# Sparse attention output with channels on partitions: three branches in one PSUM accumulation, gates applied to the probabilities

## The chip, the core and the metric

The kernel runs on one core of a Trainium2 chip. A core has five engines that matter here: TensorE (PE, matrix products and transposes; PEld is its weight load), VectorE (DVE), ScalarE (ACT), GpSimd (POOL) and SyncE (SP), which here only issues DMAs. Each engine works through its own list of instructions in order and waits on semaphores for the others. The metric is the device time of one execution in microseconds; smaller is better. Before the change the median of three runs is 2396.43 us (2393.08 to 2398.14).

## The reference, cut to what matters

The kernel computes two layers over 1024 tokens of 1024 channels, all in fp32. Layer 0 (retention and mLSTM heads) is not touched. Layer 1 has 16 heads of sparse attention (NSA, four groups of four heads, 64 channels a head) beside an S5 part. NSA has three branches: compressed blocks (c), selected blocks (s) and a window of 512 tokens (w). Each has its own softmax, and the outputs are added with a gate each, then multiplied by the output gate and sent through the output projection:

```python
p_c = jax.nn.softmax(s_c, axis=-1)
o_c = jnp.einsum('bgktj,bjgd->btgkd', p_c, vc)
...
p = jax.nn.softmax(s.reshape(b_, g, hpg, Q_BLOCK, topn * SEL_BLOCK), axis=-1).reshape(s.shape)
o_s = jnp.einsum('bgkqns,bgqnsd->bqgkd', p, v_sel)
...
p_w = jax.nn.softmax(s_w, axis=-1)
o_w = jnp.einsum('bgkqs,bsgd->bqgkd', p_w, vwb)
...
gt = jax.nn.sigmoid(gate_pre).reshape(b_, s_, g, hpg, 3)
o = gt[..., 0:1] * o_c + gt[..., 1:2] * o_s + gt[..., 2:3] * o_w
...
y_nsa = y_nsa * jax.nn.silu(nz)
mix = jnp.concatenate([y_nsa, y_s5], -1).astype(u.dtype)
return mix @ w_out
```

## The kernel before

**Products in two parts.** Each fp32 operand of a large product is split into a high part that the matrix unit takes exactly and a low part (`hi` by ACT, `lo` by a subtraction on DVE or POOL), and a product is three matmuls: high by high, high by low, low by high. `load_w` (lines 148 to 166) does this for weights: a DMA into one of two `raw` buffers, then a slot of the pool `wsp`, which has six slots of `whi` and six of `wlo`.

**Projections of layer 1.** The generator `nsa_projections` computes queries, keys, values, the branch gates and the output gate of NSA and writes them to DRAM; it yields after each group of products, and its pieces are used as work for PE inside other stages. Values are one product of 512 columns per tile of 128 tokens (8 tiles of 24 matmuls). Branch gates (48 columns) and output gate (1024 columns) are three products of 360, 356 and 356 columns per tile (`proj_tok`, L1099 to L1111): tokens on partitions. They go to DRAM as `gD` and `zD`, row by row of tokens; `gts` brings the branch gates back.

**Units.** The attention is 32 units: four groups gg of heads by eight tiles i of 128 tokens. A unit runs through these steps:

- `head` (L1310): loads the queries, computes the compressed scores (tile `cs`) and their softmax (`scc`, on DVE and ACT), the mask `mg` of the selected blocks (POOL), transposes the four heads' probabilities (`ct`, L1363), splits them (`cp`) and multiplies them with the compressed values, four matmuls of 128 columns (`co`), which ACT copies to `o6`. It is issued one unit ahead.
- `scores` (L1402) for the window and then for the selected branch: per head two matmuls for up to 512 keys (`sc`), a DVE instruction that adds the mask and finds the maximum (L1415, tiles `pr` and `nm`), and an ACT exponential that also gives the sum (L1418, `sums`). The probabilities `pr` stay unnormalised.
- `values` (L1423) for each branch: per 128 keys four transposes on PE into one PSUM tile (`pt`, L1429), a split (`pthh` by ACT, L1398; `pthl` by DVE, L1399), and two matmuls of 512 columns into the accumulator `av`, which has one buffer. Channels stand on its partitions, high and low part of the values in its halves. ACT and DVE add the halves into `ob` (L1437, L1438) at the end of each branch.
- the end of a unit: four transposes of `ob` back to tokens on partitions (`ot`, L1591), an ACT copy (L1592), a reciprocal of the eight sums and the factors `cf` (L1594 to L1597, DVE and POOL), the sum of the halves of the compressed branch (L1599, DVE), then L1600 to L1604 on POOL: two multiplications by the factors, two additions, and the product with the output gate `zn`. The result goes to DRAM as `mixN`, tokens by channels.

**Filler.** `filler` is a generator with S5's GLU (`gl`) and the output projection (`fp`, three groups of k-tiles, and the last one with the norm). `step` takes pieces from it between the steps of a unit, by credits that the table `share` sets per group. NSA tiles are read back from `mixN` and transposed (`turn`, tile `ft`, L1458), split (`fhi`, `flo`), and multiplied.

**Order.** The program is written in Python order and then put into each engine's order by a scheduler, by a simulated time of its own; so an edit moves instructions on all engines. After the units, `gate_stage` (products `gp`) ends the kernel; `late_tile` does the last NSA tile there.

Of the kernel before, what the change touches and what calls it, by code (L numbers as in the profile page):

```python
# [33 lines left out]
def shape_constants():  # L34
    """Arrays that depend on the shapes alone, packed along one row of 128 partitions."""
# [62 lines left out]
def body(tc, A, out, dbg=None):  # L98
# [69 lines left out]
    def chunk(w, segs, nkt=8, kt0=0, gain=None, pack=True):  # L168
        """[kt pair] high and low parts; four k-tiles share a slot where the columns are few"""
# [5 lines left out]
    def proj_tok(ps, uT, i, ck, n, c0=0, nkt=8, start=True, stop=True):  # L175
        """ps[tokens of tile i, n] = u @ W"""
# [9 lines left out]
    def proj_col(ps, uT, half, ck, c0, m=128, nkt=8):  # L186
        """ps[m columns, 512 tokens] = (u @ W).T"""
# [20 lines left out]
    def transpose_split(x, i, hi, lo, nk=8, off=None):  # L208
        """x [128 tokens, nk*128] -> hi/lo[:, k, tokens]"""
# [31 lines left out]
    zD = dram.tile([S, S], FT, name="zD")  # L241
    mixN = dram.tile([S, S], FT, name="mixN")
# [34 lines left out]
    # ------------------------------------------------------------- layer 1: S5 matrices of the parameters  # L277
    def s5_prepare(e):
# [43 lines left out]
        # turns by 1..8 chunks (fine) and by 0, 8, .. 120 chunks (rough); sines of the lower half negated  # L322
# [10 lines left out]
        def rotate(oc, os, xc, xs, yc, ys, tmp):  # L333
            """(oc, os) = (xc, xs) turned by (yc, ys)"""
# [7 lines left out]
        def double(X, o, m, n):  # L342
            """entries o+n.. o+n+m-1 = entries o .. o+m-1 turned by entry o+n-1"""
# [14 lines left out]
        # (abar - 1) / a  # L358
# [13 lines left out]
        # B and i*B, stacked [re; im]  # L372
# [17 lines left out]
        # C, conjugated and stacked: cc = [re; -im], jc = [-im; -re]  # L390
# [68 lines left out]
    # ------------------------------------------------------------- layer 0: retention heads  # L459
# [8 lines left out]
    def halve(hi, lo, src, eng=v):  # L468
        """src as exact high and low parts"""
# [11 lines left out]
    def gate_z(z_ps, dst):  # L481
        """dst = z*(1+tanh(z/2)) = 2*silu(z)"""
# [3 lines left out]
    def values_in(ck, n, extra=None):  # L486
        """the value rows' parts, tile by tile"""
# [16 lines left out]
    def cell(c, scf, q, kz, vc, st, n, decay):  # L504
        """one chunk: its output in PSUM and the next state"""
# [20 lines left out]
    def retention_head(h):  # L526
# [43 lines left out]
        # mix  # L570
# [134 lines left out]
    def mlstm_keys(h):  # L705
        """queries and keys after the convolution"""
# [19 lines left out]
    def mlstm_head(h, qk, V):  # L726
# [44 lines left out]
        # gates of the cell's output and of the head  # L771
# [75 lines left out]
    def square_weights(w, ext, gain=None, kt0=0, nkt=8):  # L847
        """[col half][kt pair] slots of nkt*128 rows of a 1024-column matrix"""
# [6 lines left out]
    def in_pairs(front, proj, after=None, order=tuple(range(NT))):  # L855
        """Tiles two by two, the left column halves first; a tile's front runs a tile or two ahead."""
# [21 lines left out]
    def out_stage(pw, src, w, kt0, ext, gain, sink, nkt=8, after=None):  # L878
        """sink(i, half, psum) for src @ (gain * w[kt0*128..])"""
# [14 lines left out]
    def post_norm(pw, i, y, gpost, resid, dst):  # L894
        """dst rows = resid rows + rmsnorm(y) * gpost"""
# [10 lines left out]
    def gate_stage(pw, layer, ext, src, dst, nxt=None, ppD=None, order=tuple(range(NT)), ph=None, late=()):  # L906
        """dst = h + sigmoid(h Wg) * (p Wp); with nxt, also the next layer's normalised input"""
# [55 lines left out]
        def turn(i):  # L963
            """the next layer's input: norm of tile i, transposes of tile i - 1"""
# [716 lines left out]
```

## Time and profile before

| what | value |
|---|---|
| time, median of 3 runs | 2396.43 us |
| span of the profiled execution | 2390.1 us |
| PE busy in it | 2311.4 us (97%) |
| DVE, ACT, POOL busy | 1448.3, 1047.9, 426.3 us |
| attention stage, 1567 to 2278 us | 711 us, PE busy 674.05 us |

The span is the time from the first to the last instruction of one execution that the hardware profiler took; the runs' times are measured from outside and are some 6 us longer. "Busy" of PE is the time covered by matmul records. These records include the time a matmul takes to drain, so that they overlap: the true cost of one matmul in a dense stretch is the distance from its start to the start of the next. A row of the time line gives a start, a duration and a count; the distance of two rows' starts divided by the count is that cost.

### The profile page before, as it was taken

The numbers are of one execution on the slowest core, as the hardware profiler recorded it, in microseconds if no ns is written. First come the engines' busy times: TensorE is split into PE (matmuls) and PEld (weight loads), VectorE is DVE, ScalarE is ACT, GpSimd is POOL, SyncE is SP. The second block draws the span as 40 slices with busy tenths as digits, with TensorE's granted clock in tenths as the row PEclk, the third lists the DMA queues.
The fourth block names the chain that finished last, engine by engine and source line by source line (L and its number), as shares of the span: only waits on it lengthen the run. The fifth ranks groups of instructions, "written<-read, shape, count | busy, mean of one in ns | idle before, by whom it ended". The sixth has DMA issues, their size and how long they took to land. (4 is left out here: it accounts for less than half of the span.)

```text
span 2390.1 us, 34752 instructions
## 1 busy us (share of the span) xinstructions
PE 2311.4 (97%) x12230; PEld 1940.6 (81%) x12230; DVE 1448.3 (61%) x3760; ACT 1047.9 (44%) x2271; POOL 426.3 (18%) x618
## 2 busy tenths in 40 slices
PE   7999999999999999899999999989999999999888
PEld 6878789788887888788888868979888888887767
DVE  6777647755554334343387332357768878898933
ACT  6233323433332331223332212256777877777821
POOL 0122200000000000100000000023444244445610
PEclk9999999999999999999999999999999999999999
DMA  5323312021111645314377412452363353435542
GB/s 158 90 80 103 100 45 71 27 80 35 55 57 50 242 153 213 112 69 132 116 224 240 118 46 102 121 150 76 106 188 119 99 158 102 137 120 174 165 139 112
DMA packets 255609, 279.69 MB, mean 117 GB/s; under 512 B 54688, under 2 KB 190344, under 8 KB 255402
## 3 DMA queue, kind: packets, MB, share of 16 engines
q1 hardware_dynamic: 242858, 242.05, 32.8%
q10 hardware_dynamic: 8960, 26.49, 3.2%
q0 software_dynamic: 3616, 8.92, 1.3%
q8 instruction: 97, 1.59, 0.3%
q14 instruction: 78, 0.64, 0.1%
HBM read 190.03 MB, written 88.62 MB: 117 GB/s over the span
## 5 line engine op out<-in xcount | busy, mean ns | idle before, releaser
L139 PE MATMUL pj<-whi,uh 128*128 128x512 f32 (+2 forms) x768 | 278.5, 363 | 2.6 <-ACT whi L163 1.1
L139 PE MATMUL pj<-wlo,uh 128*128 128x512 f32 (+2 forms) x768 | 277.7, 362 | 0.0
L139 PE MATMUL pj<-whi,ul 128*128 128x512 f32 (+2 forms) x768 | 277.7, 362 | 0.0
L1418 ACT ACTIVATE pr<-pr,nm 128x640 f32<-128x640 f32 (+7 forms) x256 | 187.7, 734 | 44.3 <-DVE nm L1415 43.4
L1399 DVE TENSOR_TENSOR pthl<-pt,pthh 128x512 fp32r<-128x512 f32 x264 | 176.4, 683 | 20.1 <-ACT pthh L1398 18.7
L164 DVE SCALAR_TENSOR_TENSOR wlo<-raw,gnp,whi 128x512 fp32r<-128x512 f32 (+4 forms) x248 | 142.3, 610 | 72.8 <-ACT whi L163 70.2
L139 PE MATMUL gp<-whi,mhl 128*128 128x512 f32 x512 | 167.8, 403 | 7.0 <-DVE mhl L219 4.9
L163 ACT ACTIVATE whi<-raw,gnp 128x512 fp32r<-128x512 f32 (+4 forms) x248 | 135.2, 605 | 75.7 <-PE pj L139 38.8
L139 PEld LDWEIGHTS pj<-whi,uh 128*128 128x128 f32 x768 | 145.6, 190 | 26.0 <-ACT whi L163 1.4
L139 PE MATMUL op<-whi,mhl 128*128 128x512 f32 x520 | 165.0, 395 | 0.9 <-ACT mhl L218 0.9
L1398 ACT ACTIVATE pthh<-pt 128x512 fp32r<-128x512 f32 x264 | 150.8, 594 | 32.3 <-PE pt L1429 28.2
L1429 PE MATMUL pt<-consts,pr 128*128 128x128 f32 x1056 | 157.0, 275 | 7.8 <-ACT pr L1418 6.1
L139 PEld LDWEIGHTS pj<-wlo,uh 128*128 128x128 f32 x768 | 145.7, 190 | 22.8 <-issue 0.7
L139 PEld LDWEIGHTS pj<-whi,ul 128*128 128x128 f32 x768 | 145.3, 189 | 22.3 <-issue 0.2
L139 PE MATMUL pj<-vh,whi 128*128 128x512 f32 x384 | 153.0, 399 | 0.2 <-ACT vh L218 0.2
L1429 PEld LDWEIGHTS pt<-consts,pr 128*128 128x128 f32 x1056 | 128.9, 142 | 29.5 <-ACT pr L1418 7.8
L139 PE MATMUL pj<-vl,whi 128*128 128x512 f32 x384 | 151.4, 394 | 0.0
L139 PE MATMUL pj<-vh,wlo 128*128 128x512 f32 x384 | 150.8, 393 | 0.0
L139 PE MATMUL sc<-kh,q 128*128 128x320 f32 (+5 forms) x384 | 139.3, 366 | 5.8 <-DVE nm L1415 5.3
L139 PE MATMUL sc<-kl,q 82*128 82x320 f32 (+5 forms) x384 | 126.3, 332 | 0.0
L139 PEld LDWEIGHTS gp<-whi,mhl 128*128 128x128 f32 x512 | 97.3, 191 | 29.5 <-DVE mhl L219 5.4
L139 PE MATMUL av<-pthl,vt 128*128 128x512 f32 x264 | 112.8, 427 | 4.1 <-DVE pthl L1399 3.6
(439 smaller groups left out, 5658.0 us busy)
## 6 DMA issues: line engine op xcount, KB each, us to landing
raw<-in_ab_w_in_dram SPq DMA_DIRECT2D x100, 256.0 KB
yD<-fy SPq DMA_DIRECT2D x48, 256.0 KB
raw<-in_cd_w_in_dram SPq DMA_DIRECT2D x20, 512.0 KB
raw<-in_ab_w_out_dram SPq DMA_DIRECT2D x16, 512.0 KB
raw<-in_pe_gate_dram SPq DMA_DIRECT2D x16, 512.0 KB
qD<-qst SPq DMA_DIRECT2D x16, 512.0 KB
q<-qD SPq DMA_DIRECT2D x32, 256.0 KB
fin<-yD SPq DMA_DIRECT2D x32, 256.0 KB
```

The source lines that it names most:

```text
L139: return t.matmul(o, l, r, start=start, stop=stop, **k)
L163: s.activation(hi[:, k], raw[:, k], AF.Copy, scale=gain(kt0 + k))
L164: v.scalar_tensor_tensor(lo[:, k], raw[:, k], gain(kt0 + k), hi[:, k].bitcast(FT), op0=OP.mult, op1=OP.subtract)
L1398: s.activation(hi[:dst_shape], ps[:dst_shape], AF.Copy)
L1399: v.tensor_tensor(lo[:dst_shape], ps[:dst_shape], hi[:dst_shape].bitcast(FT), op=OP.subtract)
L1418: s.activation(pr[:, :nk], pr[:, :nk], AF.Exp, scale=-1.0, bias=nm[:, c:c + 1], accum_out=sums[:, b, h:h + 1])
L1429: t.transpose(ps[:, h * 128:(h + 1) * 128], P[h][:, k * 128:(k + 1) * 128], ident)
```

## The change

The output of a unit stays with channels on partitions, and all three branches are added up in `av`.

- The probabilities are scaled before the transposes: `scale` (new) takes the reciprocal of the four sums of a branch and multiplies by the gate (two DVE instructions on 128x4), then POOL multiplies each head's `pr` by its factor, in place. There are 256 such POOL instructions, 128 to 1024 columns wide, 135168 columns in all. The compressed probabilities are multiplied by their gate on POOL (`sg`).
- The four `co` matmuls and their ACT copy become one matmul of 512 columns that opens the accumulation in `av`; `values` of both branches add to it. The halves are added once, 64x256 twice where it was 64x512 twice.
- `ot`, its ACT copy, L1594 to L1597 and L1599 to L1603 are gone. The product with the output gate remains.
- `zD` and `mixN` are channels by tokens. The output gate is computed with channels on partitions (`proj_col`, two chunks of 512 columns, 384 matmuls of 512 columns); the branch gates come with the selected values (304 columns), window values apart (256 columns), and stay in SBUF (`gates`, no `gD`).
- The filler reads `mixN` with channels on partitions already, so `turn` goes away for NSA tiles: it splits straight from SBUF (ACT and POOL). It now waits in its generator until the units it reads are written.
- Two heads are issued at other places (n in (3, 8) for (3, 11)), the first group of keys at n == 11, and `share` is {30, 26, 20, 64} for {30, 30, 28, 66}.

```diff
+            sg = nh.tile([128, 4, 64], FT, name="sg", tag="sg", bufs=1)
+            g.tensor_tensor(sg, sc, gate_of(gg, i)[:, 0, :, None].to_broadcast([128, 4, 64]), op=OP.mult)
...
-            ps = pC.tile([128, 512], FT, name="co", tag="pc")
-            for h in range(4):
-                hs = slice(h * 128, (h + 1) * 128)
-                mm(ps[:, hs], pc2[:, hs], vcT[:, gg, :], True, True)
-            s.activation(o6[:, 0].rearrange("p h d -> p (h d)"), ps, AF.Copy)
-            return q2, q3, o6, mg
+            return q2, q3, pc2, mg
...
+        def scale(P, nk, b, sums, gv):
+            cf = nh.tile([128, 4], FT, name="cf", tag="cf", bufs=4)
+            v.reciprocal(cf, sums[:, b])
+            v.tensor_tensor(cf, cf, gv[:, 1 + b], op=OP.mult)
+            for h in range(4):
+                g.tensor_scalar(P[h][:, :nk], P[h][:, :nk], cf[:, h:h + 1], None, op0=OP.mult)
...
-                T = turn(x, 2)
+                T = local_parts(x, 2, g)
...
             Pw = scores(K[1], q2, q3, i, 1, None, sums)
+            scale(Pw[0], Pw[2], 1, sums, gv)
             step(gg, nw / 2)
             Ps = scores(K[0], q2, q3, i, 0, mg, sums)
+            scale(Ps[0], Ps[2], 0, sums, gv)
             step(gg, ns / 2)
-            values(K[1], *Pw, ob, 1)
+            acc = pV.tile([128, 512], FT, name="av", tag="av")
+            mm(acc, vcT[:, gg, :], pc2, True, False)
+            values(K[1], *Pw, acc, False)
             step(gg, nw / 2)
-            values(K[0], *Ps, ob, 0)
+            values(K[0], *Ps, acc, True)
             step(gg, ns / 2)
-            ps = pT.tile([128, 512], FT, name="ot", tag="pt")
-            for h in range(4):
-                t.transpose(ps[:, h * 128:(h + 1) * 128], ob[:, h * 128:(h + 1) * 128], ident)
...
+            for b, here, there in ((0, lo_, up), (1, up, lo_)):
+                s.activation(oc[here], a4[there, :, b], AF.Copy)
+                v.tensor_tensor(ob[here], a4[here, :, b], oc[here], op=OP.add)
+            (g if n + 1 < len(units) else v).tensor_tensor(zt, zt, ob, op=OP.mult)
```

How this moves instructions is shown at two places. The first is PE at the end of a unit. Before, a unit's end reads like this (`ot` are the transposes back, `pt` those of the next unit's probabilities, `ft` the filler's, `ct` the compressed branch's):

```order
L1458 MATMUL ft_18009<-consts_75,fin_18007 128x128 x2
L1363 MATMUL ct_18074<-consts_75,scc_18049 64x128 x4
L139 MATMUL sc_18151<-kh_14698,q2_17693 128x448
L139 MATMUL sc_18151<-kl_14699,q3_17694 128x448
L139 MATMUL sc_18158<-kh_14698,q2_17693 128x448
L139 MATMUL sc_18158<-kl_14699,q3_17694 128x448
L1591 MATMUL ot_18016<-consts_75,ob_17750 128x128 x4
L1429 MATMUL pt_18209<-consts_75,pr_18091 128x128
```

In the changed program the same place has no `ot`; three `pt` tiles of the window are filled head by head, the next unit's scores (`sc`, `cs`) and the filler (`fp`) stand between, and the accumulation `av` opens with one matmul of the compressed branch (`cp` by `vcT`):

```order
L1438 MATMUL pt_17726<-consts_75,pr_17625 128x128
L1438 MATMUL pt_17737<-consts_75,pr_17625 128x128
L1438 MATMUL pt_17748<-consts_75,pr_17625 128x128
L139 MATMUL sc_17938<-kh_14645,q2_17552 128x320
L139 MATMUL sc_17938<-kl_14646,q3_17553 128x320
L139 MATMUL fp_16936<-whi_16880,fhi_16896 128x512
L139 MATMUL sc_17942<-kh_14645,q2_17552 128x320
L139 MATMUL sc_17942<-kl_14646,q3_17553 128x320
L139 MATMUL cs_17891<-kcH_12067,q2_17886 128x64
L139 MATMUL av_17724<-cp_17285,vcT_12069 128x512
```

The transposes of the sum left PE's row, and the transposes of the probabilities (`pt`) now read what POOL has scaled. The second place is POOL in the middle of a unit of the third group. Before, its row holds the mask `mg` and the end of the unit (`o6`, `zn`):

```order
L1358 COPY mg_17410<-i2_17407 128x640
L1359 TENSOR_TENSOR mg_17410<-i2_17407,c_scaus_12058 128x128
L1600 TENSOR_TENSOR o6_17377<-o6_17377,cf_17749 128x4x64
L1601 TENSOR_TENSOR o6_17111<-o6_17111,cf_17428 128x512
L1602 TENSOR_TENSOR o6_17111<-o6_17111 128x4x64
L1596 COPY cf_18089<-gts_12071 128x4
L1345 MEMSET im_18972 128x18
L1603 TENSOR_TENSOR o6_17111<-o6_17111 128x4x64
```

In the changed program it holds the scaling of the window's four heads and of the selected branch's four heads, with two weight splits (`wlo`) and the output gate's product (`zn`) between them:

```order
L1365 TENSOR_TENSOR mg_17589<-i2_17586,c_scaus_12057 128x128
L1431 TENSOR_SCALAR pr_17603<-pr_17603,cf_17647 128x640
L1431 TENSOR_SCALAR pr_17614<-pr_17614,cf_17647 128x640
L1431 TENSOR_SCALAR pr_17625<-pr_17625,cf_17647 128x640
L1431 TENSOR_SCALAR pr_17636<-pr_17636,cf_17647 128x640
L160 TENSOR_TENSOR wlo_16881<-raw_16879,whi_16880 128x1024
L160 TENSOR_TENSOR wlo_16887<-raw_16885,whi_16886 128x1024
L1607 TENSOR_TENSOR zn_17236<-zn_17236,ob_17543 128x256
L1431 TENSOR_SCALAR pr_17663<-pr_17663,cf_17707 128x768
L1431 TENSOR_SCALAR pr_17674<-pr_17674,cf_17707 128x768
```

POOL was at the end of a unit's chain; now it stands in the middle, between the exponentials and PE's transposes.

## Rows read from the trace of the kernel before

**Rows 1.** The page's busy time of each engine: us, share, instructions.

```profile
PE 2311.4 (97%) x12230; PEld 1940.6 (81%) x12230; DVE 1448.3 (61%) x3760; ACT 1047.9 (44%) x2271; POOL 426.3 (18%) x618
```

**Rows 2.** Busy time of engines in the attention stage; clock, DMA share, GB/s.

```profile
1567.00:2278.00 711.00, 674.05 (x4087) 576.34 (x4086) 580.99 (x1688) 530.96 (x1158) 310.72 (x390) 0.98 0.44 135
```

**Rows 3.** PE's waits in that stage: us in total, times, longest us.

```profile
PE ot L1591 <- DVE ob L1438: 6.2, 7, 2.0
PE pt L1429 <- ACT pr L1418: 6.1, 5, 4.9
...
PE co L139 <- DVE cp L1366: 3.1, 2, 2.1
```

**Rows 4.** Time line of PE inside units: start us, us, instruction, count.

```profile
1818.81 0.64 PE L139 MATMUL co<-vcT,cp 128*128 128x128 f32 x4
1819.29 0.41 PE L1458 MATMUL ft<-consts,fin 128*128 128x128 f32 x2
1819.45 0.39 PE L139 MATMUL sc<-kh,q 128*128 128x320 f32 x1
...
1825.19 0.39 PE L139 MATMUL av<-pthh,vt 128*128 128x512 f32 x1
1825.42 0.40 PE L139 MATMUL av<-pthl,vt 128*128 128x512 f32 x1
...
1831.44 0.66 PE L1591 MATMUL ot<-consts,ob 128*128 128x128 f32 x4 [0.29 <-DVE ob L1438]
1831.94 1.04 PE L1429 MATMUL pt<-consts,pr 128*128 128x128 f32 x8
```

**Rows 5.** Time line of PE in dense products of 512, 356, 256 columns.

```profile
1440.15 0.40 PE L139 MATMUL pj<-whi,vh 128*128 128x512 f32 x1
...
1445.76 0.40 PE L139 MATMUL pj<-whi,vh 128*128 128x512 f32 x1
...
1554.75 0.33 PE L139 MATMUL pj<-whi,vl 128*128 128x356 f32 x1
...
1558.67 0.33 PE L139 MATMUL pj<-whi,vl 128*128 128x356 f32 x1
...
1598.65 0.28 PE L139 MATMUL gl<-flo,whi 128*128 128x256 f32 x1
...
1599.96 0.28 PE L139 MATMUL gl<-fhi,whi 128*128 128x256 f32 x1
```

**Rows 6.** POOL's groups by shape: count, busy us, mean ns of one.

```profile
L1519 POOL TENSOR_TENSOR fy<-fy,fin 128x512 f32<-128x512 f32 x32 | 41.2, 1287 | 80.8 <-ACT fy L1515 78.5 <-DVE scc L1337 2.3
...
L1602 POOL TENSOR_TENSOR o<-o 128x256 f32<-128x256 f32 x31 | 22.9, 738 | 1.6
...
L1358 POOL COPY mg<-i 128x896 f32<-128x896 f32 x4 | 3.7, 930 | 0.4 <-DVE i L1354 0.2
...
L1358 POOL COPY mg<-i 128x256 f32<-128x256 f32 x4 | 1.6, 397 | 0.3
```

**Rows 7.** DVE's and ACT's groups by shape, on the units' path.

```profile
L1438 DVE TENSOR_TENSOR ob<-av,oc 64x512 f32<-64x512 f32 x64 | 44.0, 687 | 9.7 <-ACT oc L1437 8.4
L1415 DVE CUSTOM_DVE_ANT_0 pr<-sc,c_wmask,nm 128x320 f32<-128x320 f32 x64 | 34.8, 543 | 7.3 <-PE sc L139 6.4
...
L1447 DVE TENSOR_TENSOR flo<-ft,fhi 128x256 fp32r<-128x256 f32 x23 | 9.5, 415 | 0.4 <-ACT fhi L1446 0.3
...
L1334 DVE RECIPROCAL m<-m 128x4 f32<-128x4 f32 x32 | 5.5, 171 | 0.5
...
L1418 ACT ACTIVATE pr<-pr,nm 128x640 f32<-128x640 f32 x80 | 66.3, 828 | 21.5 <-DVE nm L1415 21.2
L1418 ACT ACTIVATION_READ_ACCUMULATOR pr<-pr,nm 128x1 f32 x256 | 49.2, 192 | 0.0
```

**Rows 8.** DVE on tile cf (durations min/median/max ns), POOL on line 160 (mean ns).

```profile
L1597 DVE TENSOR_TENSOR cf<-sums,gts x32: 130/168/1734, 1589.8 to 2264.6; 128x8 f32<-128x8 f32 x32
...
L160 POOL TENSOR_TENSOR wlo<-raw,whi 128x1024 fp32r<-128x1024 f32 x20 | 47.5, 2384 | 66.8 <-PE sc L139 38.1 <-ACT whi L159 24.0 <-PE gl L139 2.6
```

More of the change, by code (lines that the diff above doesn't have):

```diff
@@ L240, in body @@
     aqD = dram.tile([NA, 16, S], FT, name="aqD")
-    zD = dram.tile([S, S], FT, name="zD")
-    mixN = dram.tile([S, S], FT, name="mixN")
+    zD = dram.tile([8, 128, S], FT, name="zD")
+    mixN = dram.tile([8, 128, S], FT, name="mixN")
     mixS = dram.tile([512, 8, 128], FT, name="mixS")
@@ L1048, in body @@
     NL = 1
-    gD = dram.tile([128, 8, 48], FT, name="gD")
     uD = dram.tile([512, 8, 128], FT, name="uD")
@@ L1054, in body @@
     pz = [(psA, "psA")]
+    gates = [None]
     def nsa_projections(pd):
@@ L1431, in values @@
                 vb = K[2][:, k0 // 128 + k, :]
-                mm(acc, vb, hi, k == 0, False)
-                pace[0] = mm(acc, vb, lo, False, k == n - 1)
-            lo_, up = slice(0, 64), slice(64, 128)
-            here, there = (up, lo_) if b else (lo_, up)
-            oc = n2.tile([128, 512], FT, name="oc", tag="oc", bufs=1)
-            s.activation(oc[here], acc[there], AF.Copy)
-            v.tensor_tensor(ob[here], acc[here], oc[here], op=OP.add)
+                mm(acc, vb, hi, False, False)
+                pace[0] = mm(acc, vb, lo, False, last and k == n - 1)
         def filler():
@@ L1496, in filler @@
                                               (A["p"][1, 0], A["pe_proj"][1], 0, 2, ppD, False),
[L1497 to L1498 removed]
+                                              (mixN, W2, 0, 4, yD, True),
+                                              (mixN, W2, 4, 2, yD, True)):
                 wq = weights(w, kt0, nk)
                 for i in range(NT):
+                    while src is mixN and not all((q, i) in ready for q in ((0, 1) if kt0 == 0 else (2,))):
+                        yield
                     x = ftile()
[L1502 to L1506 removed]
+                    to = dst[i * 128:(i + 1) * 128, :]
+                    if src is None or src is mixN:
+                        x = x.rearrange("p (a k) -> p a k", a=4)[:, :nk]
+                        if src is None:
+                            to = dst.rearrange("(k l) c -> l k c", l=8)[i]
+                            nc.sync.dma_start(x, mixS[:, i, :].rearrange("(a p) k -> p a k", p=128))
+                        else:
+                            nc.sync.dma_start(x, mixN[kt0:kt0 + nk, :, i * 128:(i + 1) * 128].rearrange("a p k -> p a k"))
+                        T = local_parts(x, nk, g)
                     else:
[L1508 removed]
                         nc.sync.dma_start(x[:, :nk * 128], src[i * 128:(i + 1) * 128, :])
@@ L1554, in body @@
         credit, pace = [0.0], [None]
-        share = {0: 30, 1: 30, 2: 28, 3: 66}
+        share = {0: 30, 1: 26, 2: 20, 3: 64}
         ready = {}
@@ L1590, in body @@
-            for h in range(4):
-                t.transpose(ps[:, h * 128:(h + 1) * 128], ob[:, h * 128:(h + 1) * 128], ident)
-            s.activation(o6[:, 1].rearrange("p h d -> p (h d)"), ps, AF.Copy)
-            gv = gts[:, i, 12 * gg:12 * gg + 12].rearrange("p (h b) -> p b h", b=3)
-            v.reciprocal(sums, sums)
-            ge = g if n + 1 < len(units) else v
-            g.tensor_copy(cf[:, 0, :], gv[:, 0, :])
-            v.tensor_tensor(cf[:, 1:3, :], sums, gv[:, 1:3, :], op=OP.mult)
@@ L1605, in body @@
+            (g if n + 1 < len(units) else v).tensor_tensor(zt, zt, ob, op=OP.mult)
             if gg < 3 or i in LAST[-NL:]:
-                nc.sync.dma_start(mixN[rows, cols], zt)
+                nc.sync.dma_start(mixN[2 * gg:2 * gg + 2, :, rows].rearrange("a p k -> p a k"), zt)
             ready[gg, i] = zt
@@ L1609, in body @@
             pass
-    if dbg is not None and dbg["stop"] in ("nsa", "mix1"):
-        nc.sync.dma_start(dbg["o"][:, :1024], mixN)
-        if dbg["stop"] == "mix1":
-            nc.sync.dma_start(dbg["o"][:, 1024:], mixS.rearrange("c l k -> (k l) c"))
-        ctx.close()
-        return
     ep.close()
@@ L1625, in late_tile @@
             rows = slice(i * 128, (i + 1) * 128)
-            x = pw.tile([128, 256], FT, name="lx", tag="lx")
-            nc.sync.dma_start(x, mixN[rows, 768:])
+            x = pw.tile([128, 2, 128], FT, name="lx", tag="lx")
+            nc.sync.dma_start(x, mixN[6:8, :, rows].rearrange("a p k -> p a k"))
             nc.sync.dma_start(y, yD[rows, :])
```

94 lines of the change are left out of this document (42 added, 52 removed).

## The prediction

> **What bounds the kernel now.** I read the page's busy times first: PE is busy 97% of the span, no other engine over 61% (PEld overlaps PE) [rows 1]. So PE is the bound over the whole kernel, and what counts is how many microseconds of PE an edit takes away or makes wait. The change lies in the attention stage and in the projections ahead of it, so the stage's own row comes next: 711 us, PE busy 674, DVE 581, ACT 531, POOL 311, clock 0.98 of full [rows 2]. PE has 37 us idle there; DVE is at 82% and is the engine to watch after PE. Which waits make up the 37 us is in PE's waits: 6.2 us at `ot`, which waits for DVE's `ob`, 3.1 at `co`, which waits for `cp`, 6.1 at `pt`, of which 4.9 is one wait [rows 3]. No wait has a large share: the stage is bound by PE's own work, with many small waits.
>
> The price of one PE instruction must not be taken from mean durations, since records overlap; I take the distance of starts in dense stretches. Four `co` take 0.48 us (1818.81 to 1819.29), two `ft` 0.16, four `ot` 0.50 (1831.44 to 1831.94), one `av` of 512 columns 0.23 [rows 4].
>
> **What leaves and joins PE.** Four sums, each from counts of instructions and the distances of [rows 4].
> `ot`: 128 transposes in 32 sets of four, 32 x 0.50 = 16.0 us less.
> `co`: 128 matmuls, 32 x 0.48 = 15.4 us less.
> `ft`: the filler's transposes fall from 78 to 16 (the p part keeps them), 31 pairs x 0.16 = 5.0 us less.
> `av`: 32 matmuls of 512 columns join, 32 x 0.23 = 7.4 us more.
> Net 29.0 us less. Weight loads go with their matmuls and need no term of their own.
>
> **Projections.** Before: 576 matmuls of 356 or 360 columns and 192 of 512. 24 matmuls of 356 take 3.92 us (1554.75 to 1558.67), 0.163 each; 24 of 512 take 5.61 us, 0.234 each [rows 5]: 576 x 0.163 + 192 x 0.234 = 138.8 us. After: 384 of 512, 192 of 304, 192 of 256. 11 matmuls of 256 take 1.31 us, 0.119 each [rows 5]; for 304 I go along the line between 256 and 356 and take 0.140. That is 384 x 0.234 + 192 x 0.140 + 192 x 0.119 = 139.6 us. The difference, +0.8 us, I count as nothing. The value chunks now hold all six weight slots (four for the 304 columns, two for the 256), so the next chunk's first slot comes free only in the last tile, with 18 + 24 matmuls (5.4 us by the prices above) still to run there. Its DMA lands in a `raw` buffer beforehand; what is left to do is ACT's and DVE's split. I count nothing, and a few us if that cover is too short.
>
> **Waits that go.** `ot` and `co` waits (6.2 + 3.1 = 9.3 us) [rows 3] go with the instructions. The engines that were late there may be late for the next piece, so between 0 and 9.3; I take 7, since DVE and ACT both lose work too: DVE's `ob` halves shrink from 64 x 687 ns to about 64 x 415 (the 256-column subtraction from PSUM is the nearest row), 17 us less, the filler's splits of 256 columns (415 each) go to POOL, and 64 reciprocals at 171 ns and 64 products at 168 (median of `cf`) come, 22 us more [rows 7, 8]. ACT loses two copies of 512 columns a unit.
>
> **The new link: POOL between exponential and transpose.** The trace of before has no POOL multiplication by a factor per partition. Its nearest rows are the copy `mg` with one input, 397 ns at 256 columns and 930 at 896, so 0.18 us + 0.83 ns a column, and the instructions with two inputs, 738 ns at 256 and 1287 at 512, so 0.19 us + 2.14 ns a column [rows 6]. For 256 instructions and 135168 columns that is 46 + 113 = 159 us or 49 + 290 = 339 us. I take the first: the factor is one number per partition, and only one tensor is read. The Trainium skill bears on the choice in "GPSIMD Engine Reference", section 3.1: its measured model has about 1.03 cycles an element for short one-input bodies and 2.5 as the floor for two inputs. By that page POOL's share stays as taken here; if the factor counted as a second input, the dear price would hold.
>
> POOL then does, in this stage, 311 us, less L1600 to L1603 (about 4 x 22.9 = 92, each taken as L1602), plus 159, plus `sg` (32 x 0.74 = 24), plus the filler's splits (8 x 1.29 + 15 x 0.74 = 21): 423 us, about 63% of a stage of 675. At the dearer price it is 603 us, 89%. POOL is not the bound at either.
>
> So what matters is delay. From a branch's last score to its first transposition a chain must run: DVE's maximum 0.54, ACT's exponential and its sum 0.83 + 0.19, reciprocal 0.17, factor 0.17 [rows 7, 8], POOL 0.71 for 640 columns: 2.6 us, where it was 1.6; each further head adds 0.71. Against it stands PE's own work between these two instructions, which I get from the order of the changed program with the distances above: over the 64 branches it is 3.5 to 17 us, median 9 us; before it was as little as nothing and 6 us in the median. The last head's first transposition comes later still, 6 us or more. Head by head, no branch falls short with the cheap price, so the sum gets no term for it. If that cover were gone, each branch would cost PE up to 2.6 + 2.1 us, 64 x 4.7 = 300 us; so the cover is what the forecast rests on.
>
> What is queued behind: POOL is in order, so a scaling can stand behind a weight split of 2.38 us [rows 8]. With one such split ahead of every group, the shortfall by the same count is 4 us in all with the cheap price and 27 with the dear one.
>
> **DMA.** `zn` and `mixN` move in pieces of 512 bytes instead of 1024, same bytes. DMA is busy 0.44 of the stage [rows 2], and a tile is loaded a unit ahead: nothing. At the kernel's end the last unit loses its transposes and four DVE steps ahead of the store, but PE waits there for other loads: nothing.
>
> **Sum.** 2390.1 - 29.0 + 0 - 7 = 2354.1 us of span. The runs' median stood 6.3 us above the profiled span; I keep that: 2360 us. Differences within 0.2% (4.8 us) can't be told from no change here.
>
> **Rivals.**
> *More waits go than these.* The other 28 us of PE's idle time are waits for DVE and ACT, and both lose work while the cover of a branch grows from 6 to 9 us. If half to three quarters go: 14 to 21 us more, 2339 to 2346. For it: the order. Against it: DVE is at 82%, and in a shorter stage hardly lower. Chance 0.22, at 2342.
> *POOL holds up DVE.* A DVE product of two SBUF operands on 128x8 took 130 ns at best and 1734 at worst [rows 8], while POOL was running. `head` has some twelve such small instructions a unit, `cf` now two sets more, and POOL's share rises from 44% to 63%. If each of 16 such instructions in 32 units waits 0.05 us more on average, DVE loses 26 us; as DVE feeds PE, most of it returns as PE waits: 2360 + 16 to 2360 + 36, and at the upper end nothing is left of the gain. The Trainium skill, "SBUF — State Buffer", section "Who interferes with whom", calls the pair of ports that DVE and POOL share an exclusive lock, held for a whole instruction; the 1734 ns agree, and by that rule a 0.71 us scaling holds a small DVE instruction up less long than a 2.38 us split does. Against this rival: DVE's two dearest groups (`pthl`, the maximum) read PSUM. Chance 0.18, at 2385.
> *Slower: the chain through POOL takes PE's place.* If scaling costs the dear price (1.56 us for 640 columns, four heads 6.2 us), and 4.4 us of other POOL or DVE work stands ahead of each group (a split and two filler instructions), 35 of the 64 branches outlast their cover and PE loses 75 us: 2360 + 75 = 2435. It decides from 36 us, 0.56 us a branch, on. Against it: the price, for which the row with one input speaks. Chance 0.08.
>
> **How the numbers follow.** The forecast has 0.52, its own range 2350 to 2374 (waits -9 to 0, projections up to +5, cover short by 4, spread of the prices). With the rivals: faster by over 0.2% is 0.52 + 0.22 + 0.10 of the second rival = 0.84; within 0.2% 0.08 (the rest of the second); slower 0.08. The range for 8 in 10 runs from 2336 (below the first rival) to 2394 (the second in full); it leaves out the third rival and the tails.
>
> **What would show it.** `ot` and `co` gone from PE and the stage some 35 us shorter, with the time ahead of it and after it unchanged: the main term. A POOL scaling of 640 columns near 0.71 us: the price; near 1.56, the dear one. PE's waits at `pt` still under some 10 us in all: the cover holds; tens of us at `pt` for POOL: the third rival. DVE's small instructions much longer, and PE waiting more at `sc` and `av`: the second. PE's idle time in the stage under 20 us: the first. I would be wrong altogether if the scheduler's order, made with a simulated time, leaves PE waiting at places that neither trace nor order shows.

## The result, and the profile after

The changed kernel takes 2540.36 us (median of 4 runs, 2533.18 to 2542.03); beside it the kernel before took 2395.28. The ratio on record is 1.0588, with a 95% interval of 1.0572 to 1.0604; the two medians alone give 1.061. The kernel is slower by 145 us, where 2360 us was forecast. The forecast was wrong in its sign.

First the page of the kernel after, and the row of its attention stage, from the first score to the first `trp`, the transposes with which `gate_stage` begins (us, busy time of PE, PEld, DVE, ACT and POOL with counts, clock, DMA share, GB/s).

```profile
PE 2375.2 (94%) x11942; PEld 1934.8 (76%) x11942; DVE 1438.4 (57%) x3765; ACT 1013.0 (40%) x2215; POOL 764.9 (30%) x773
```

```profile
1567.00:2431.00 864.00, 740.76 (x3802) 579.91 (x3801) 573.90 (x1696) 496.12 (x1096) 651.36 (x548) 0.90 0.37 111
```

Against [rows 1] PE has 288 instructions fewer and is busy 64 us more; POOL went from 426 to 765 us. Against [rows 2] the stage went from 711 to 864 us, and that is the whole loss: the first score starts at 1566.69 us (1567.16 before), and what follows the stage takes 109 us (112.5 before). Inside it PE's idle time grew from 37 to 123 us. The other 67 us are in PE's busy time, although work left PE: the granted clock is 0.90 instead of 0.98. How much of the 67 us is the clock was not measured. POOL is at 75%, from 44%.

The price that the forecast had to guess: the scalings on POOL, by shape (count, busy us, mean ns of one, idle time ahead).

```profile
L1431 POOL TENSOR_SCALAR pr<-pr,cf 128x640 f32<-128x640 f32 x80 | 149.4, 1886 | 49.8 <-DVE cf L1429 31.7 <-ACT pthh L1400 10.8 <-DMA fin<-yD 5.2
...
L1431 POOL TENSOR_SCALAR pr<-pr,cf 128x1024 f32<-128x1024 f32 x16 | 45.4, 2860 | 2.6 <-PE pt L1438 2.6
...
L1431 POOL TENSOR_SCALAR pr<-pr,cf 128x128 f32<-128x128 f32 x32 | 18.7, 602 | 9.8 <-ACT pr L1420 9.0 <-DVE cf L1429 0.4
```

From 128 to 1024 columns that is 0.28 us + 2.52 ns a column: 1.89 us for 640 columns, dearer than both ends of the bound (0.71 and 1.56, from [rows 6]). All 256 take 407 us.

Where does PE lose its time? Here are waits in the stage, by engine (us in total, times, longest us).

```profile
PE fp L139 <- DVE fy L1545: 20.7, 9, 8.2
PE sc L139 <- DVE nm L1417: 19.6, 37, 3.2
PE av L139 <- ACT pthh L1400: 17.0, 29, 1.9
PE cs L139 <- DMA q<-qD: 10.7, 9, 2.6
...
PE cs L139 <- DMA q<-aqD: 8.5, 12, 1.7
...
PE pt L1438 <- POOL pr L1431: 2.5, 2, 2.3
...
PEld sc L139 <- DVE nm L1417: 61.0, 126, 3.5
...
DVE pr L1417 <- PE sc L139: 46.6, 59, 4.5
...
DVE pr L1417 <- PE pt L1438: 32.4, 33, 3.1
...
ACT pthh L1400 <- PE pt L1438: 96.2, 93, 5.0
```

Two of these waits in the stage of the kernel before:

```profile
DVE pr L1415 <- PE pt L1429: 8.4, 8, 2.2
...
ACT pthh L1398 <- PE pt L1429: 28.2, 42, 2.9
```

And the chain that ended last in the kernel after, over its whole span, by engine:

```profile
PE 80%; DVE 7%; DMA 6%; issue 2%; ACT 2%; SPq 2%; POOL 0%; ACTq 0%; DVEq 0%; POOLq 0%
```

Here the page misleads. PE waits at `pt` for POOL for 2.5 us in all, the chain gives POOL 0%, and the waits name DVE and ACT, neither of which became busier (574 and 496 us in the stage, 581 and 531 before). They wait in their turn for PE's transposes: ACT 96 us for `pt` (28 before), DVE 32 us for a buffer of probabilities that `pt` has yet to free (8 before). It looks like a ring in which POOL is the slow member and everybody else is seen waiting; the experiments have to show whether it is. A stretch of POOL's time line:

```profile
2016.43 0.72 POOL L1607 TENSOR_TENSOR zn<-zn,ob 128x256 f32<-128x256 f32 x1
2020.30 6.19 POOL L1431 TENSOR_SCALAR pr<-pr,cf 128x512 f32<-128x512 f32 x4 [3.15 <-DVE cf L1429]
...
2026.55 1.27 POOL L1528 TENSOR_TENSOR fy<-fy,fin 128x512 f32<-128x512 f32 x1
2027.78 1.27 POOL L1451 TENSOR_TENSOR flo<-fin,fhi 128x512 fp32r<-128x512 f32 x1
2029.01 1.36 POOL L1528 TENSOR_TENSOR fy<-fy,fin 128x512 f32<-128x512 f32 x1
2034.40 0.62 POOL L1368 TENSOR_TENSOR sg<-scc,gts 128x256 f32<-128x256 f32 x1 [4.03 <-DVE scc L1343]
2035.30 6.18 POOL L1431 TENSOR_SCALAR pr<-pr,cf 128x512 f32<-128x512 f32 x4 [0.28 <-DVE cf L1429]
```

One branch holds POOL for 6.2 us. Between two branches POOL works off what piled up meanwhile, then stands idle for 3 to 4 us for the next input: its queue is in order, and the next entry isn't ready. Whether POOL's load, the price in the chain, or the mere extra step costs the time, these rows can't say.

### The profile page after: what moved, and what is told of

Same layout as the page of the kernel before. It is cut to its first block, busy times and chain, and to the rows that moved or that the text cites. A ratio compares the mean times of both kernels' runs of the same rounds, so it can differ in the third digit from the quotient of the medians.

```text
span 2540.1 us, 34650 instructions
## 1 busy us (share of the span) xinstructions
PE 2375.2 (94%) x11942; PEld 1934.8 (76%) x11942; DVE 1438.4 (57%) x3765; ACT 1013.0 (40%) x2215; POOL 764.9 (30%) x773
## 4 chain that ended last, share of the span: by engine, by line
PE 80%; DVE 7%; DMA 6%; issue 2%; ACT 2%; SPq 2%; POOL 0%; ACTq 0%; DVEq 0%; POOLq 0%
PE pj L139 37%; PE gp L139 7%; PE op L139 7%; PE av L139 5%; PE fp L139 5%; PE sc L139 4%; PE pt L1438 4%; PE yp L139 2%; DVE pr L1417 2%; PE gl L139 2%; PE trp L214 2%; PE hp L139 1%; DMA q<-aqD 1%; PE cs L139 1%; DVE pthl L1401 1%
## 5 line engine op out<-in xcount | busy, mean ns | idle before, releaser
L1431 POOL TENSOR_SCALAR pr<-pr,cf 128x640 f32<-128x640 f32 (+7 forms) x256 | 406.7, 1606 | 90.4 <-DVE cf L1429 51.5
L139 PE MATMUL pj<-vh,whi 128*128 128x512 f32 x512 | 203.5, 398 | 0.2 <-ACT vh L218 0.2
L139 PE MATMUL pj<-vh,wlo 128*128 128x512 f32 x512 | 202.2, 395 | 0.1
L139 PE MATMUL pj<-vl,whi 128*128 128x512 f32 x512 | 201.0, 393 | 0.0
L1438 PE MATMUL pt<-consts,pr 128*128 128x128 f32 x1056 | 188.9, 294 | 3.0 <-POOL pr L1431 2.5
L164 DVE SCALAR_TENSOR_TENSOR wlo<-raw,gnp,whi 128x512 fp32r<-128x512 f32 (+3 forms) x248 | 142.3, 611 | 77.4 <-ACT whi L163 76.5
L1438 PEld LDWEIGHTS pt<-consts,pr 128*128 128x128 f32 x1056 | 145.6, 152 | 32.0 <-issue 5.9
L163 ACT ACTIVATE whi<-raw,gnp 128x512 fp32r<-128x512 f32 (+3 forms) x248 | 135.1, 605 | 80.2 <-PE pj L139 37.4
L226 POOL TENSOR_TENSOR rsb<-rsa,mhalf 128x1 f32<-128x1 f32 x32 | 17.7, 552 | 407.3 <-DVE rsa L224 407.3
L139 PE MATMUL av<-pthl,vt 128*128 128x512 f32 x264 | 127.6, 483 | 11.0 <-DVE pthl L1401 10.3
```

The lines of the kernel that those rows point to most:

```text
L139: return t.matmul(o, l, r, start=start, stop=stop, **k)
L163: s.activation(hi[:, k], raw[:, k], AF.Copy, scale=gain(kt0 + k))
L164: v.scalar_tensor_tensor(lo[:, k], raw[:, k], gain(kt0 + k), hi[:, k].bitcast(FT), op0=OP.mult, op1=OP.subtract)
L1431: g.tensor_scalar(P[h][:, :nk], P[h][:, :nk], cf[:, h:h + 1], None, op0=OP.mult)
L1438: t.transpose(ps[:, h * 128:(h + 1) * 128], P[h][:, k * 128:(k + 1) * 128], ident)
```

## The experiments

All runs start from the changed kernel, and the scheduler made each one's order anew: in every one POOL's instructions stand in another order than in the changed kernel. I had four theories. **Price**: the scaling's duration in the chain from exponential to transposition. **Link**: the extra step in that chain, whatever it takes. **Load**: 407 us more on POOL, in the way of its other work. **Rest**: the other parts of the change.

**The scaling left out, and cut to 64 columns.**

```diff
-            for h in range(4):
-                g.tensor_scalar(P[h][:, :nk], P[h][:, :nk], cf[:, h:h + 1], None, op0=OP.mult)
```

> The changed kernel with the 256 scalings on POOL left out (the probabilities go unscaled into the transposes; reciprocal and factor are still made). Four theories. Price: the scaling's duration (0.28 us + 2.51 ns a column, 407 us in all) in the chain from exponential to transposition makes the loss; link: the extra engine and wait in that chain, and the order the scheduler makes around it, cost the time whatever the duration; load: POOL's 407 us more stand in the way of its other work and of DVE's SBUF operands; rest: the other parts of the change cost it (filler without its transposes, gates in SBUF, one accumulation, weight slots). Price, link and load all expect 2350 to 2370 us (the forecast of 2360 without the link), clock back at 0.98 in the stage. Rest expects over 2450.

2360.45 us, 0.9842 of before (0.9827 to 0.9856). The rest theory falls: the loss hangs on the scalings. The stage of this run:

```profile
1564.00:2250.00 686.00, 652.93 (x3804) 554.31 (x3802) 538.97 (x1696) 487.42 (x1096) 252.06 (x292) 0.97 0.46 138
```

```diff
-                g.tensor_scalar(P[h][:, :nk], P[h][:, :nk], cf[:, h:h + 1], None, op0=OP.mult)
+                g.tensor_scalar(P[h][:, :64], P[h][:, :64], cf[:, h:h + 1], None, op0=OP.mult)
```

> The changed kernel with every scaling cut to the first 64 columns of its head (the other columns stay unscaled): the same 256 instructions, waits and links to the first transposition of a branch, at about 0.28 + 0.16 = 0.44 us each, 113 us in all. Price: within 15 us of the run without scalings, 2355 to 2380 us. Load: the same, since 294 us of POOL's load are gone. Link: over 2460, since the chain is as long in engines as in the changed kernel.

2381.34 us (ratio 0.9933, 0.9916 to 0.9950). One scaling takes 443 ns:

```profile
L1431 POOL TENSOR_SCALAR pr<-pr,cf 128x64 f32<-128x64 f32 x256 | 107.9, 443 | 127.7 <-DVE cf L1429 60.1 <-PE fp L139 13.0 <-ACT pthh L1400 12.3
```

That is 1 us above the range of price and load. So the link with 108 us of load costs 21 us, and most of the 180 us between 2360 and 2540 hang on the scaling's duration. The link theory alone, which expected over 2460, falls. Price and load both stand.

**Another form at a lower price.**

```diff
-                g.tensor_scalar(P[h][:, :nk], P[h][:, :nk], cf[:, h:h + 1], None, op0=OP.mult)
+                g.tensor_tensor(P[h][:, :nk], P[h][:, :nk], cf[:, h:h + 1].to_broadcast([128, nk]), op=OP.mult)
```

> The changed kernel with the scaling written as a product of two tensors on POOL, the factor broadcast along the columns (the form that before's L1600 and L1601 have: 615 ns at 256 and 1061 at 512 columns, so 0.17 us + 1.74 ns a column, 1.28 us for 640, 279 us in all where the one with a factor per partition took 407). If the form keeps that price: price and load expect a loss that falls with the duration, 2400 to 2480 us; link expects 2520 to 2545. If the broadcast form is as dear as the other here, 2540 by every theory.

2434.78 us (1.0157, 1.0142 to 1.0173). The product of two tensors is cheaper than the one with a factor per partition, 1.27 against 1.89 us for 640 columns, 267 us in all:

```profile
L1431 POOL TENSOR_TENSOR pr<-pr,cf 128x640 f32<-128x640 f32 x80 | 98.9, 1267 | 47.4 <-DVE cf L1429 37.9 <-PE sc L139 5.0 <-ACT pthh L1400 2.3
```

More than half of the loss goes with a third of the duration. It has a price of its own: DVE's products of two SBUF operands take longer. First its row in the run without scalings, then in the changed kernel, then here (count, busy us, mean ns):

```profile
L1337 DVE TENSOR_TENSOR scc<-scc,m 128x192 f32<-128x192 f32 (+7 forms) x30 | 11.6, 385 | 0.2
```

```profile
L1337 DVE TENSOR_TENSOR scc<-scc,m 128x192 f32<-128x192 f32 (+7 forms) x30 | 13.2, 441 | 0.6
```

```profile
L1337 DVE TENSOR_TENSOR scc<-scc,m 128x192 f32<-128x192 f32 (+7 forms) x30 | 25.3, 844 | 0.6
```

Summed over DVE's groups in the stage, the same 1696 instructions last 626 us without scalings, 640 in the changed kernel and 658 here.

**Load without link.** The scalings stay, in number, form and width, though not at the same places in POOL's queue, but work on a tile that nobody reads.

```diff
+        junk = np_.tile([128, S], FT, name="junk", tag="junk", bufs=1)
+        g.memset(junk, 0.0)
...
-                g.tensor_scalar(P[h][:, :nk], P[h][:, :nk], cf[:, h:h + 1], None, op0=OP.mult)
+                g.tensor_scalar(junk[:, :nk], junk[:, :nk], cf[:, h:h + 1], None, op0=OP.mult)
```

> The changed kernel with the 256 scalings kept in number, form, width and place in POOL's queue, with the same factors, but working on a tile that nobody reads: the probabilities stay unscaled, and no transposition waits for POOL. POOL's load stays at 407 us more. Load expects 2480 to 2545 us. Price and link expect 2355 to 2395 (POOL's other work, such as weight splits and the products with zn, may still come late behind it).

2515.55 us (1.0497, 1.0474 to 1.0519). No transposition waits for a scaling directly, and 155 of the 180 us are still there, as load expected. But the kernel still waits for POOL in other ways: DVE for one of the four tiles for factors, PE behind it for an exponential, and PE at the end for the load of `h`, the rows that `trp` transposes.

```profile
DVE cf L1431 <- POOL junk L1434: 40.4, 8, 16.0
```

```profile
PE pt L1441 <- ACT pr L1423: 44.0, 8, 18.9
PE trp L214 <- DMA h<-hD: 40.3, 1, 40.3
```

So the next run has 16 tiles for factors:

```diff
-            cf = nh.tile([128, 4], FT, name="cf", tag="cf", bufs=4)
+            cf = nh.tile([128, 4], FT, name="cf", tag="cf", bufs=16)
```

> The run whose scalings work on a tile that nobody reads (2515 us), with 16 tiles for the factors instead of 4. There DVE still waited 40 us for POOL to be done with a factor, so POOL could fall behind by two units only. If the loss of 155 us came back through the factors' ring: 2360 to 2430 us. If it came through POOL's other work standing late behind the scalings (filler, weight splits, products with zn): 2480 to 2520.

2523.03 us (1.0518, 1.0503 to 1.0533), 3 above the range of the second expectation and far from the first. The trace tells another story than either. The stage, PE's wait at its end, and POOL's time line there (`fy` is the filler's output):

```profile
1564.00:2413.00 849.00, 661.36 (x3815) 552.58 (x3813) 551.24 (x1696) 487.23 (x1096) 659.35 (x548) 0.89 0.39 116
```

```profile
PE trp L214 <- DMA h<-hD: 134.2, 1, 134.2
```

```profile
2290.68 2.48 POOL L1559 TENSOR_TENSOR fy<-fy,fin 128x512 f32<-128x512 f32 x2
2293.13 107.35 POOL L1434 TENSOR_SCALAR junk<-junk,cf 128x1024 f32<-128x1024 f32 x62
```

PE goes through the units as fast as without scalings: its last transposition of probabilities starts at 2241.6 us (2243.2 without). So with almost nobody waiting for it, the load does not slow the units. POOL does not keep up. At 2293 us it still has 117 us of scalings ahead of it, of which the row shows 62, and its last one ends at 2410.4. Then the load of `h` is issued, for which PE had stood idle since 2279.7 us, 34 us later than the same wait begins without scalings; that the load waits for the scratch tile's memory is inferred, from the two times. By that inference most of this run's 163 us is a wait that the scratch tile itself makes, and what the run shows is POOL's pace: in its order POOL needs until 2410 us for its 659 us of work, even if nobody waits for a scaling. Where it stands idle on the way is at its other work, not at the scalings (2.1 us):

```profile
POOL wlo L160 <- ACT whi L159: 42.9, 5, 28.8
POOL sg L1368 <- DVE scc L1343: 29.7, 19, 4.9
POOL zn L1610 <- DVE ob L1609: 27.6, 15, 4.2
...
POOL junk L1434 <- DVE cf L1432: 2.1, 1, 2.1
```

In the changed kernel the last scaling starts at 2379.6. There the probabilities can't be left behind, so PE is held to POOL's pace all along instead of at the end.

**Less load, link and price kept.** The filler's sums and products on POOL (76 instructions) are left out.

> The changed kernel without the filler's sums and products on POOL (the products with z5 and the gain, the sums with the parts of yD and the residual: 76 instructions, 92 us; left out). The 256 scalings, their duration and their link stay. If POOL's load counts (652 us, against 680 that PE alone needs): the loss of 180 us falls by 50 to 110 us, 2430 to 2490. If the length of the chain from exponential to transposition counts (a scaling of 1.6 us itself): less than 25 us, over 2515.

2477.49 us (1.0333, 1.0320 to 1.0347): 63 us back for 85 us of POOL's time in the stage (651 to 567), with every scaling as long as before and still waited for: in the range of load, and not in that of the chain. But only 30 us of it come back in the units (last transposition at 2358.9 us instead of 2388.7). The other 33 come back behind them, where the edit also takes the sums out of the filler's own chain, so that they need not be load.

**More buffers.**

```diff
-                pr = np_.tile([128, (S, 640)[b]], FT, name="pr", tag=f"pr{b}", bufs=(5, 4)[b])
+                pr = np_.tile([128, (S, 640)[b]], FT, name="pr", tag=f"pr{b}", bufs=(6, 6)[b])
```

> The changed kernel with six buffers for each branch's probabilities instead of five (selected keys) and four (window). In the trace of after DVE's maxima wait 32 us for transpositions, that is for a buffer of probabilities to come free. If the delay comes back through these buffers: 20 to 60 us faster than the changed kernel, 2480 to 2520. If POOL is simply too full (652 us of work against a stage of 680 that PE alone would need), within 10 us of 2540.

2516.04 us (1.0502, 1.0487 to 1.0518), 24 us back: in the range of the buffers, and outside the 10 us that a POOL simply too full would leave. So POOL's share has no hard limit, it rose from 75 to 77%, and part of the delay returns to DVE by way of the buffers; the other 156 us do not.

Put side by side (stage from the first score to the first `trp`, the row of engines by stretch; the last column is when the last transposition of probabilities starts, so what comes after it is no longer the units'):

| run | stage, us | POOL busy, us | share | time, us | last `pt`, us |
|---|---|---|---|---|---|
| no scaling | 686 | 252 | 37% | 2360 | 2243 |
| 64 columns | 710 | 356 | 50% | 2381 | 2267 |
| two-input form | 756 | 512 | 68% | 2435 | 2302 |
| filler left out | 803 | 567 | 71% | 2477 | 2359 |
| six buffers | 839 | 650 | 77% | 2516 | 2373 |
| no link, 4 factors | 840 | 658 | 78% | 2516 | 2362 |
| no link, 16 factors | 849 | 659 | 78% | 2523 | 2242 |
| changed kernel | 864 | 651 | 75% | 2540 | 2389 |

The four runs in which POOL has 650 us of work or more have stages of 839 to 864 us, with link or without, with more buffers or without. The rows above them get dearer the fuller POOL is. POOL's queue stops at 75 to 78% in these orders.

The last column splits the loss. Of the changed kernel's 180 us, 146 arise in the units (2389 against 2243) and 35 behind them: from the last `pt` to the first `trp` 42 us pass, where it was 7.5 without scalings and 9.6 with the filler's sums left out. There the filler works off what it has left, and PE's longest wait is the one at `fp` for `fy`. The chain of that stretch runs through DMAs of `hD` and `yD` and the sums on POOL.

**The scalings on other engines.** First all on DVE, then shared.

```diff
-                g.tensor_scalar(P[h][:, :nk], P[h][:, :nk], cf[:, h:h + 1], None, op0=OP.mult)
+                v.tensor_scalar(P[h][:, :nk], P[h][:, :nk], cf[:, h:h + 1], None, op0=OP.mult)
```

> The changed kernel with all 256 scalings on DVE instead of POOL, same form (before has 128x1024 with a factor per partition at 746 ns and 128x256 with two of them at 408, so about 0.29 us + 0.45 ns a column: 0.58 us for 640, 135 us in all). If POOL's slowness at this work is the cause, wherever it is waited for, the loss of 180 us goes and what is left is DVE's own limit: 577 us (its busy time in the stage without scalings) + 135 = 712 us of a stage that PE alone would end in about 680: 2385 to 2430 us. If the link costs by itself (one more step between exponential and transposition), over 2450.

2440.03 us (1.0184, 1.0167 to 1.0201), 10 over the range: the scalings took 145 us instead of 135, and DVE came to 86% of a stage of 769 us. So 100 of the 180 us come back. That DVE is now too full is likely, and the runs that share the work bear it out. The 577 us of DVE and 507 of ACT that this expectation and the next ones start from belong to a window that runs on past the stage; in the stage without scalings they are 539 and 487, so the sums made from them are some 20 to 40 us too high.

```diff
+                if h in (0, 2):
+                    s.activation(P[h][:, :nk], P[h][:, :nk], AF.Copy, scale=cf[:, h:h + 1])
+                else:
+                    (g if h in () else v).tensor_scalar(P[h][:, :nk], P[h][:, :nk], cf[:, h:h + 1], None, op0=OP.mult)
```

(`h in ()` never holds, so these are on DVE.)

> The changed kernel with the scalings shared, heads 1 and 3 on DVE, heads 0 and 2 on ACT as a copy with a factor per partition (like the exponential without its sum, 829 ns for 640 columns). DVE 577 + 68 = 645 us, ACT 507 + 94 = 601 us of a stage of about 680; POOL back at 253. Price and load, wherever they are waited for: 2365 to 2400 us, so at or under the kernel before. Link by itself: over 2430.

2403.96 us (1.0028, 1.0016 to 1.0040), 4 over the expected range: 136 of the 180 us come back, 44 are left over the run without scalings. With head 0 on POOL in the two-input form, heads 1 and 2 on ACT and head 3 on DVE:

> The changed kernel with the scalings shared over three engines: head 0 on POOL in the two-input form (1.27 us for 640 columns, measured), heads 1 and 2 on ACT, head 3 on DVE. POOL 253 + 67 = 320 us, ACT 507 + 94 = 601, DVE 577 + 34 + some 10 of being held up by POOL's two-input products = 620. 2362 to 2395 us if each engine's load counts; within 10 us of the run with DVE and ACT, or above it, if the slowest link of a branch (1.27 us on POOL) counts.

2409.40 us (1.0059, 1.0037 to 1.0080), worse by 5, as the slowest link of a branch expected and not as each engine's load did. A second cause, not told apart from it, is in DVE's scalings. First the run with DVE and ACT, then this one:

```profile
L1434 DVE TENSOR_SCALAR pr<-pr,cf 128x640 f32<-128x640 f32 (+7 forms) x128 | 74.2, 618 | 1.0
```

```profile
L1436 DVE TENSOR_SCALAR pr<-pr,cf 128x640 f32<-128x640 f32 (+4 forms) x64 | 57.1, 893 | 1.1
```

Half as many take 893 ns each instead of 618 with POOL's products beside them, so POOL's share relieved DVE by 17 us and not by 37. With DVE and ACT again, and six buffers; then heads 0 to 2 on ACT and head 3 on DVE, six buffers; then of that the window's head 3 on POOL in the two-input form:

> The run with the scalings shared between DVE (heads 1, 3) and ACT (heads 0, 2), which took 2404 us, with six buffers for each branch's probabilities as well. Its DVE waited 10 us for such a buffer, and PE 34 us (at weight loads) for DVE's maxima. If buffers give the slack back here as they did in the changed kernel (24 us of 180): 2385 to 2398 us, at or just under the kernel before. If DVE's load (647 us of about 700) sets this run: within 5 us of 2404.

> The same with heads 0 to 2 on ACT and head 3 on DVE: DVE 577 + 37 = 614 us, ACT 507 + 130 = 637. If DVE's load sets the run before: 2375 to 2392 us. If two engines near 90% each of a stage are as bad either way round: 2395 to 2415.

> The run with heads 0 to 2 on ACT, head 3 on DVE and six buffers (2396 us), with head 3 of the window branch moved from DVE to POOL in the two-input form: DVE 614 - 18 = 596 us, POOL 253 + 32 = 285 with room to spare. If DVE's load is what is left of the cost: 2380 to 2392 us, under the kernel before. If ACT's load (637 us), the chain, or DVE being held up by POOL's two-input products set it: 2392 to 2405.

2404.25 us (1.0025, 1.0015 to 1.0035), 2395.64 (0.9990, 0.9979 to 1.0001) and 2394.45 (0.9990, 0.9977 to 1.0002). Buffers gave nothing, as DVE's load expected; taking load off DVE gave 9 us, in the range of two full engines being as bad either way round and not in that of DVE's load; the last step gave nothing that can be told apart, also in the second range. The last two are level with the kernel before. No version that scales all the probabilities beats it.

**What is left of the 44 us.** The shared scalings of the run with 2404 us, put on two tiles that nobody reads:

```diff
+                if h in (0, 2):
+                    s.activation(junk[0][:, :nk], junk[0][:, :nk], AF.Copy, scale=cf[:, h:h + 1])
+                else:
+                    v.tensor_scalar(junk[1][:, :nk], junk[1][:, :nk], cf[:, h:h + 1], None, op0=OP.mult)
```

> The run with the scalings shared between DVE (heads 1, 3) and ACT (heads 0, 2), 2404 us, but with the scalings working on two tiles that nobody reads, and 16 tiles for the factors: the same load on DVE and ACT, no transposition waits for a scaling (the probabilities stay unscaled). If the 44 us that this sharing still costs over the kernel without scalings (2360) are DVE's and ACT's load: 2390 to 2405 us. If they are the longer chain from exponential to transposition: 2360 to 2375.

2379.89 us (0.9930, 0.9918 to 0.9943), between the two expectations: 19 us are load (2360.45 to 2379.89) and 24 the longer chain (to 2403.96), if the 16 tiles for factors, which this run has and that one hasn't, change nothing. With 64 columns on POOL chain and load together cost 21 us. For the full width on POOL no run gives the chain's price, since the runs without link wait for POOL in other ways.

## Why the prediction was wrong, step by step

- **PE's work, -29.0 us, and waits, -7**: right in direction, about two thirds there in size. Without scalings the kernel runs in 2360.45 us, the very time forecast, but by luck: its stage is 24 us shorter and not the 36 of the sum, and 7 more come in about equal parts ahead of it and behind it, where the forecast saw no change. Its span is 2359.2 us (forecast 2354.1), and its median stood 1.2 us above that instead of 6.3; the 6.3 was mostly spread between runs, since each run's own span lies some 2 us under its time (2359.2 under 2361.28 here). `ot` and `co` are gone from PE.
- **Projections, nothing**: right within the spread of single executions; the first score starts 0.5 us earlier in the changed kernel, 3.2 without scalings.
- **POOL's price, 0.71 us for 640 columns, 1.56 at the dear end**: wrong, the first failing term. It is 1.89. I took the nearest row to be one with a single tensor read; the measurement is on the other side of the two-input rows of [rows 6], and a true two-input product is cheaper, 1.27. The Trainium skill, "GPSIMD Engine Reference", section 3.1, on which I had leaned, orders the forms the other way: 1.03 cycles an element for short bodies, about 2.6 for a product of two tensors. By that rule, if the factor is no second input, the factor form would be the cheaper one. The trace disagrees: 1886 against 1267 ns.
- **"POOL is not the bound at either"**: wrong, and the decisive step. I set POOL's 603 us against 675 and read 89% as room. Some 650 us on POOL went with stages of 839 to 864 us in all four runs that have them, with POOL idle 22 to 25% of the time at entries that weren't ready. I looked at delay per branch against its cover only, never at whether the queue drains. That PE's 146 us in the units are this pace and not the delay of each branch is likely, from the run in which POOL needs until 2410 us with nobody waiting; it is not shown apart from the chain.
- **The chain, no term, as PE's own work covers it**: wrong, by 24 us with the scalings on DVE and ACT, and by at most 21 with 64 columns on POOL. The cover I counted was PE work in program order, as if it were always ready; a likely reason, not tested, is that this work waits for DVE and ACT itself.
- **"PE's waits at `pt` still under some 10 us: the cover holds"**: a bad sign to choose. They are 2.5 us for POOL, and the kernel is slower all the same. The loss stands in waits at `sc`, `av`, `fp` and `cs`, and in PE's busy time at the lower clock.
- **Rival: the chain through POOL takes PE's place**, 2435 us at the dear price of 339 us, with a chance of 0.08: right in direction, but its sign, tens of us at `pt` for POOL, did not show. That the kernel took 2435 us with the two-input form is luck, since the price there was 267 us; at the true 407 it took 105 more. The rival counted missed covers and not POOL's pace.
- **Rival: POOL holds up DVE**: there, at half its size. DVE's instructions last 14 us longer in all than without scalings, where 26 were put in; with the two-input form 33.
- **DMA, nothing**: not quite. PE waited 19 us at `cs` for the DMAs of queries, where it was 1.7 before and 7.2 without scalings, and DMAs stand in the chain behind the units. Whether this only follows from POOL's delay was not tested.

What stays open: how far another order of POOL's queue would lift its 75 to 78%, which was not tried, how much the new order in each run moved its time, and how POOL's pace and the longer chain share the loss at full width.

## What to carry to other kernels

When work moves to an engine with room, add up its whole work for the stage and hold it against the share that an in-order queue fed by others can reach, here 75 to 78% in the orders that ran, and not against 100%. A price that no row shows belongs in the range on both sides of its nearest rows, and the decision should survive the dear end. A full engine need not show up in the waits: take its load away, or put it where nobody waits for it, see what the time does, and look in that trace for what still waits.

## What was not expected of the hardware

- On POOL, multiplying by a factor per partition took 0.28 us + 2.52 ns a column, and the product with the factor broadcast as a second tensor 0.18 us + 1.69 (399 ns at 128 columns, 1910 at 1024). On DVE the first form took 647 ns for 640 columns, on ACT a copy with a factor 820 (in the runs with all scalings on DVE, and with DVE and ACT).
- POOL's two-input products went with longer DVE instructions than its scalings by a factor did: with 267 us of the one DVE's instructions lasted 33 us longer in all, with 407 us of the other 14. The Trainium skill, "SBUF — State Buffer", section "Who interferes with whom", has a DVE instruction with two SBUF inputs contend with any POOL instruction that reads SBUF. The trace agrees with both forms; that one costs three and a half times as much per microsecond of POOL, the page doesn't say.
- With PE kept waiting in small pieces the granted clock of the stage fell from 0.98 to 0.90, and PE's busy time rose by 67 us with less work in it.
